# The up product of layer 0 at the front of the program, and a second early part of the output projection

## The chip, the cores and the metric

The kernel runs on one core of one Trainium2 chip. A core has TensorE (PE: matmuls, and PEld: the loads of their stationary operands), VectorE (DVE), ScalarE (ACT), GpSimd (POOL) and SyncE (SP, which here issues most DMAs); matmuls write to PSUM, everything else lives in SBUF. The metric is the device time of one execution in microseconds (us), as the median of several.

## The reference

One step of a two-layer encoder trunk over 1024 prompt tokens and 32 sample tokens, 1024 channels wide. Layer 0 is a Mamba-2 mixer (in projection, causal convolution, chunked scan in 8 groups, gate, group norm, output projection), layer 1 latent attention. Behind each mixer stands a term of per-layer embeddings p:

```
hn = rmsnorm(h, ln_w)                       # layer 0: the input x
proj = hn @ in_w                            # z, x/B/C, dt of the scan
y = ssd_scan(...) ; y = rmsnorm((y + D*xs) * silu(z))     # per group
h = h + y @ out_w
g = sigmoid(rmsnorm(h, norm_w) @ gate_w)
h = h + (p[i] @ up_w) * g
```

The product `p[0] @ up_w` ("the up product of layer 0") depends on inputs alone. Its result is first used when the gate of layer 0 is known.

## The kernel before

All tensors are held channel by token: 128 channels on the partitions, tokens along the free dimension. A product of two fp32 tensors is made of three matmuls: each operand is split into a high part h (rounded to the type fp32r, ScalarE or VectorE) and a low part l (the rest, VectorE or GpSimd), and `gemm` (L209) runs wh x ah, wh x al, wl x ah for every block of 128 channels. A weight block is loaded and split by `load_weight` (L192): a DMA into the tile `wraw`, `wh` by a cast (on ScalarE, or on VectorE where `eng_h` is given), `wl` by a subtraction on GpSimd. Each of these three tiles has two buffers in this stage.

**The order.** The program is written in Python in one order, but a planner at build time, with a model of the durations, orders the instructions of each engine by their readiness, an earlier line going first where two are ready; a tile whose buffers are all taken waits until one comes free. On the chip each engine then runs its own list in that fixed order and waits by semaphores.

**The scan stage** is `phase_ssd` (L263 to L580). At its front the input is normalized in three pieces of 384, 384 and 292 tokens (`TILES1`, index j). For each piece: four DMAs of the input into `xt` (L289), squares on ScalarE, VectorE and GpSimd, pairwise sums on VectorE (L303), four sums over the channels on TensorE (`psn`, L304), the inverse root on ScalarE (L182 and L183), then for each of eight channel blocks the product `hf` on VectorE (L311), its high part `hh` on ScalarE (L313) and its low part `hl` on GpSimd, or VectorE for two blocks of eight (L314). With j=0 also come the constants and the first two weights, `dtW` and `inW[0]` (L292), and some matmuls on constants (`busy`, L279) which only keep TensorE at work.

Then `raw_block` (L326) and `mblock` (L316) run the in projection: for each j one product of eight channel blocks for each weight, into one of three PSUM banks of the tag `mm`; ScalarE copies each out (L330). The first call takes `dtW` and `inW[0]` together (L350 and L351): "the first block". The dt chain on VectorE (L353 to L400) follows from it. After that 8 groups are scanned, with the in projections of the next group between them; `gate` (L417) forms y times silu(z) of a group, `finish` (L520) its norm: squares, sums, the root (L535) on ScalarE, the scaled y on VectorE (L538), and the store of y to DRAM (`y_d`, blocks 2g and 2g+1).

**The end of the stage** in the last group (L570 to L578): `up_product` (L229) is a generator. Its first step loads the two halves of `pT0` (128 x 1056 each) into `upr` and splits them into `upx` (tag `raw`, four of six buffers). Each further step takes one of 8 blocks of output channels: a weight (two loads of `upW0` serve four blocks each, nb=4), three pieces of 352 tokens with six matmuls each, a copy of each by ScalarE into `upe` (L252) and a store to `u_d` (L253). Its first step stands before the last gate and `finish`, the rest behind them (`run(up)`, L578).

**The output projection** is `phase_out` (L622), for two halves of 528 tokens. It loads the y of 16 channel blocks (`yraw`, L630) and splits them into `yhl`. `first` = 3 output columns are begun early, in the cuts that `early` gives: with `(8,)`, all three do blocks 0 to 8, then each of the 8 columns does what it still lacks. `part` (L643) loads the weights of a column in two halves, at block 0 and at block 8, and takes `[a - u : b - u]` of the half. Its PSUM tile `pso` spans two banks and has three buffers.

Of the kernel before, what the change touches and what calls it, by code (L numbers as in the profile page):

```python
# [10 lines left out]
F32 = mybir.dt.float32  # L11
F32R = mybir.dt.float32r
# [5 lines left out]
P = 128  # L18

T1 = 1060  # L20
RAWB = 6
# [3 lines left out]
T = 1056  # L25
# [166 lines left out]
def load_weight(c, src, nk, m, scale=None, eng_h=None, wp=None):  # L192
    nc = c.nc
    wp = wp or c.wp
    raw = wp.tile([P, nk, m], F32, tag="wraw", name="wraw")
    nc.sync.dma_start(raw, src)
    if scale is not None:
        nc.gpsimd.tensor_tensor(raw, raw, bc_last(scale, m), op=ALU.mult)
    wh = wp.tile([P, nk, m], F32R, tag="wh", name="wh", bufs=c.whb)
    wl = wp.tile([P, nk, m], F32R, tag="wl", name="wl", bufs=c.whb)  # L200
    if eng_h:
        eng_h.tensor_copy(wh, raw)
    else:
        nc.scalar.activation(wh, raw, AF.Copy)  # L204
    nc.gpsimd.tensor_tensor(wl, raw, wh.bitcast(F32), op=ALU.subtract)  # L205
    return wh, wl
# [19 lines left out]
    return c.pv[:rows, o + i : o + i + n]  # L226


def up_product(c, i, piece, raw, tiles, ps_tile, evac, nb=1):  # L229

    nc, I = c.nc, c.I
    o, n = piece
    acts = []
    for k in range(2):
        x = raw()[:, :n]
        nc.sync.dma_start(x, I[f"pT{i}"][:, k, o : o + n])
        h, l = tiles()[:, :n], tiles()[:, :n]
        split(c, h, l, x)
        acts.append((h, l))
    yield  # L240
    na = -(-n // 512)
    w_ = n // na
    for m in range(8):
        b = m % nb
        if b == 0:
            ws = load_weight(c, I[f"upW{i}"][m // 4][:, 2 * (m % 4) : 2 * (m % 4 + nb)], 2 * nb, P)
        w = [x[:, 2 * b : 2 * b + 2] for x in ws]
        u = evac()
        for a in range(na):
            ps = ps_tile()  # L250
            gemm(c, ps[:, :w_], w, acts, slice(w_ * a, w_ * a + w_))
            nc.scalar.activation(u[:, w_ * a : w_ * a + w_], ps[:, :w_], AF.Copy)  # L252
        c.store(c.u_d[i][m][:, o : o + n], u[:, :n])  # L253
        yield
# [8 lines left out]
def phase_ssd(c, ctx):  # L263
    nc, tc, I, O = c.nc, c.tc, c.I, c.O
# [12 lines left out]
    kp = es.enter_context(tc.tile_pool(name="keep", bufs=1))  # L277
    with tc.tile_pool(name="xin", bufs=2, side="right") as xp:
        def busy(x, k):  # L279

            ps = pc.tile([P, 512], F32, tag="trx", name="busy")
            for _ in range(k):
                nc.tensor.matmul(ps[:, : x.shape[-1]], c.ones, x, start=True, stop=True)

        busy(c.ones, 10)
        for j, (o, n) in enumerate(TILES1):
            xt = xp.tile([P, 8, n], F32, tag=f"xt{j}", name=f"xt{j}", bufs=1)
            for q in range(4):
                nc.sync.dma_start(xt[:, 2 * q : 2 * q + 2, :], I["xT"][:, 2 * q : 2 * q + 2, o : o + n])  # L289
            if j == 0:  # L290
                c.load_constants()
                early = [load_weight(c, I["dtW"], 8, 32, eng_h=nc.vector), load_weight(c, I["inW"][0], 8, P, eng_h=nc.vector)]  # L292
            ps = pc.tile([P, 512], F32, tag="st", name=f"psn{j}")
            for q in range(4):
                sq = [xp.tile([P, n], F32, tag="sq", name=f"sq{j}_{q}", bufs=6) for _ in range(2)]
                nc.scalar.activation(sq[0], xt[:, 2 * q], AF.Square)
                if j and q % 2:
                    nc.gpsimd.tensor_tensor(sq[1], xt[:, 2 * q + 1], xt[:, 2 * q + 1], op=ALU.mult)
                elif j == 0:
                    nc.vector.tensor_tensor(sq[1], xt[:, 2 * q + 1], xt[:, 2 * q + 1], op=ALU.mult)  # L300
                else:
                    nc.scalar.activation(sq[1], xt[:, 2 * q + 1], AF.Square)
                nc.vector.tensor_tensor(sq[0], sq[0], sq[1], op=ALU.add)  # L303
                nc.tensor.matmul(ps[:, :n], c.ones, sq[0], start=q == 0, stop=q == 3)  # L304
            r = xp.tile([P, n], F32, tag="r", name=f"r{j}")
            rsqrt(nc, c, r, ps[:, :n], 1.0 / 1024, c.eps)
            if j == 0:
                busy(r, 2)
            for k in range(8):
                hf = xp.tile([P, n], F32, tag="hf", name=f"hf{j}_{k}", bufs=3)  # L310
                nc.vector.scalar_tensor_tensor(hf, xt[:, k], pvc(c, "lnw0", k), r, op0=ALU.mult, op1=ALU.mult)  # L311
                hh, hl = hn[j][0][k], hn[j][1][k]
                nc.scalar.activation(hh, hf, AF.Copy)  # L313
                (nc.vector if k % 4 == 1 else nc.gpsimd).tensor_tensor(hl, hf, hh.bitcast(F32), op=ALU.subtract)  # L314

    def mblock(*blocks, ws=None):  # L316

# [237 lines left out]
    for g in range(G):  # L555
        scan_group(g, Ss[g])
        if g + 1 < G:
            bc_blocks(g + 1)
        if g:
            gate(g - 1, 0, Ss[g - 1])  # L560
            gate(g - 1, 1, Ss[g - 1])
        if g + 1 < G:
            x_block(g + 1, 0)
        else:
            gate(g, 0, Ss[g])
        if g:
            finish(g - 1, Ss[g - 1])
        if g + 1 < G:
            x_block(g + 1, 1)
        else:  # L570
            up = up_product(c, 0, (0, T), lambda: kp.tile([P, T1], F32, tag="cx", name="upr", bufs=6),
                            lambda: kp.tile([P, 3 + T1], F32R, tag="raw", name="upx", bufs=RAWB),
                            lambda: mm.tile([P, 512], F32, tag="mm", name="mm"),
                            lambda: kp.tile([P, T1], F32, tag="cx", name="upe", bufs=6), 4)
            next(up)
            gate(g, 1, Ss[g])
            finish(g, Ss[g])
    run(up)  # L578
    nc.sync.dma_start(O["conv_o"], conv_c.rearrange("p b s k -> p b (s k)"))
    es.close()  # L580

# [40 lines left out]
def phase_out(c, src_d, W, nkb, res, hpool, tmp, ypool, pool, first, early):  # L622

    nc = c.nc
    hs, rs = [], []
    for hf, (o, n) in enumerate(HB):
        acts = []
        for k in range(nkb):
            raw = pool.tile([P, 528], F32, tag="yraw", name="yraw", bufs=RAWY)
            nc.sync.dma_start(raw, src_d[k][:, o : o + n])  # L630
            yh, yl = (op_tile(ypool, (hf * nkb + k) % 16 < 8) for _ in range(2))
            split(c, yh, yl, raw)
            acts.append((yh, yl))
        row = []
        acc = tmp.tile([P, 528], F32, tag="acc", name="acc", bufs=2)

        group = range(0 if hf else first)
        cuts = [0, *early, nkb]
        pss = {m: mm2(c, "pso") for m in group}

        ws = {}

        def part(m, a, b):  # L643

            u = a // 8 * 8
            if a == u:
                ws[m] = load_weight(c, W[m][:, u : u + 8], 8, P)
            gemm2(c, pss[m], [x[:, a - u : b - u] for x in ws[m]], acts[a:b], first=a == 0, last=b == nkb)

        for a, b in zip(cuts[:-2], cuts[1:]):  # L650
            for m in group:
                part(m, a, b)
        for m in range(8):
            if m in group:
                part(m, *cuts[-2:])
            else:
                pss[m] = mm2(c, "pso")
                for u in range(0, nkb, 8):
                    part(m, u, u + 8)
            ps = pss[m]  # L660
            xr = pool.tile([P, 528], F32, tag="xres", name="xres", bufs=2)
            nc.sync.dma_start(xr, res[m][:, o : o + n])
            h = pool.tile([P, 528], F32, tag="hf", name="hf", bufs=2)
            nc.vector.tensor_tensor(pair(h), ps[:, :, :264], pair(xr), op=ALU.add)
            hh = hpool.tile([P, 528], F32R, tag="hH", name="hH", bufs=16)
            hl = hpool.tile([P, 528], F32R, tag="hL", name="hL", bufs=16)
            split(c, hh, hl, h)
            sumsq(c, tmp, h, acc, m == 0)
            row.append((hh, hl))
        hs.append(row)  # L670
        rs.append(lambda acc=acc: norm_r(c, tmp, acc, 1024, "r"))
    return hs, rs
# [451 lines left out]
def run(*gens):  # L1124
    for g in gens:
        for _ in g:
            pass
# [177 lines left out]
def build(tc, nc, I, O, dbg=None, ngroups=8, upto=9):  # L1305
# [4 lines left out]
    with ctx:  # L1310
# [61 lines left out]
        yp = ((ypa, 16), (ypb, 17))  # L1372
        tmp, tmp_es = pool("tmpA", "right")
        hp, hp_es = pool("hp")
        hs, rs = phase_out(c, c.y_d, I["outW"], 16, I["xres"], hp, tmp, yp, yt, 3, (8,))
        h1s = [[None] * 8 for _ in range(2)]
        accs = [None, None]

# [107 lines left out]
```

## Time and profile before

| | us |
|---|---|
| runs shown: median (lowest to highest) of 3 | 2014.39 (2013.51 to 2020.8) |
| the profiled execution | 2012.76 |
| its span, first to last instruction | 2011.0 |
| mean granted TensorE clock | 0.989 of full speed |

The profile is that of one execution; all durations below are from it. A group's row reads: line, engine, operation, output <- inputs, shapes, count | busy us, mean ns of one | idle time of the engine just before them, and what ended it. A row of the timeline reads: start, duration, engine, line, operation, tiles, count, and in brackets the engine's idle time before it with what ended it. Durations of matmuls are modelled and overlap, so TensorE's rate is read from the distance of their starts.

### The profile page before, as it was taken

To read this page: it belongs to the slowest core of one execution; us is meant where nothing else is said; L and a number is where in the kernel's file an instruction comes from. 1 tells how busy PE (TensorE), PEld (TensorE's weight loads), DVE (VectorE), ACT (ScalarE), POOL (GpSimd) and SP (SyncE) were. 2 spreads that over 40 slices of the span, in tenths; PEclk is the share of its full clock that TensorE was granted. 3 is DMA by queue.
4 is the path that set the end of the run, shared out by engine and by line. 5 is a ranking of instruction groups with operands and counts; after the bars stand their busy time and mean duration, and the time that the engine had idled before them with its cause. 6 is when DMAs were issued, how large, how long until landed. Compare 5 with 4: busy or idle time off the path is not lost. (4 is left out here: it accounts for less than half of the span.)

```text
span 2011.0 us, 32658 instructions
## 1 busy us (share of the span) xinstructions
PE 1932.2 (96%) x12871; PEld 1773.9 (88%) x12871; DVE 1282.6 (64%) x1601; ACT 1023.8 (51%) x1757; POOL 971.6 (48%) x813
## 2 busy tenths in 40 slices
PE   7989999999999999999998999999899999999999
PEld 5989899999999998999998999777777777779999
DVE  7898575858576675443267534274688787986544
ACT  4444444453545457334243432587687877754331
POOL 5433334344444444454678443122545453645772
PEclk8999999999999999999999999999999999999999
DMA  3143333334242446544333312533512221315432
GB/s 130 53 94 90 85 91 77 86 99 99 73 104 64 104 109 214 178 140 161 100 114 119 94 55 85 164 105 96 118 47 72 54 66 36 108 59 193 127 126 74
DMA packets 110730, 204.27 MB, mean 102 GB/s; under 512 B 18224, under 2 KB 60720, under 8 KB 110448
## 3 DMA queue, kind: packets, MB, share of 16 engines
q1 hardware_dynamic: 105472, 193.17, 32.5%
q0 software_dynamic: 2800, 6.91, 1.9%
q8 instruction: 101, 1.65, 0.3%
q10 hardware_dynamic: 2304, 2.10, 0.3%
q14 instruction: 53, 0.43, 0.1%
HBM read 156.81 MB, written 38.83 MB: 97 GB/s over the span
## 5 line engine op out<-in xcount | busy, mean ns | idle before, releaser
L205 POOL TENSOR_TENSOR wl<-wraw,wh 128x1024 fp32r<-128x1024 f32 (+2 forms) x185 | 374.1, 2024 | 413.7 <-ACT wh L204 371.5
L215 PE MATMUL mm<-hh,wh 128*128 128x384 f32 (+3 forms) x1176 | 386.0, 329 | 4.7 <-ACT raw L330 4.5
L215 PE MATMUL mm<-hl,wh 128*128 128x384 f32 (+3 forms) x1176 | 387.6, 330 | 0.0
L215 PE MATMUL mm<-hh,wl 128*128 128x384 f32 (+3 forms) x1176 | 385.4, 328 | 0.0
L204 ACT ACTIVATE wh<-wraw 128x1024 fp32r<-128x1024 f32 (+3 forms) x183 | 159.1, 869 | 280.8 <-PE pso L215 117.8
L215 PE MATMUL pso<-yhl,wh 128*128 128x264 f32 x1536 | 283.5, 285 | 5.6 <-ACT upe L252 2.9
L215 PEld LDWEIGHTS pso<-yhl,wh 128*128 128x128 f32 x1536 | 239.8, 189 | 7.0 <-DVE yhl L221 3.8
L215 PEld LDWEIGHTS mm<-hh,wh 128*128 128x128 f32 (+1 forms) x1176 | 220.3, 187 | 8.9 <-ACT raw L330 5.2
L215 PEld LDWEIGHTS mm<-hl,wh 128*128 128x128 f32 (+1 forms) x1176 | 220.8, 188 | 4.6 <-issue 2.4
L215 PEld LDWEIGHTS mm<-hh,wl 128*128 128x128 f32 (+1 forms) x1176 | 220.5, 187 | 4.2 <-issue 1.9
L215 PE MATMUL pso<-yhl,wl 128*128 128x264 f32 x768 | 219.3, 286 | 4.1 <-POOL wl L205 4.1
L413 DVE SCALAR_TENSOR_TENSOR cx<-raw,pv,cx 128x1060 f32<-128x1060 f32 x96 | 132.6, 1381 | 88.3 <-ACT cx L411 87.6
L215 PE MATMUL psi<-yhl,wh 128*128 128x264 f32 (+1 forms) x896 | 167.0, 287 | 3.9 <-ACT yhl L220 3.8
L215 PEld LDWEIGHTS pso<-yhl,wl 128*128 128x128 f32 x768 | 145.2, 189 | 4.7 <-POOL wl L205 4.7
L488 POOL TENSOR_TENSOR hm<-hT,cd_all 128x256 f32<-128x256 f32 x64 | 67.6, 1057 | 165.5 <-DVE hT L490 100.7
L215 PE MATMUL pg<-hH,wl 128*128 128x264 f32 x512 | 145.9, 285 | 0.7 <-POOL wl L205 0.7
L215 PE MATMUL pg<-hH,wh 128*128 128x264 f32 x512 | 145.9, 285 | 0.0
L215 PE MATMUL pg<-hL,wh 128*128 128x264 f32 x512 | 145.7, 285 | 0.0
L215 PEld LDWEIGHTS psi<-yhl,wh 128*128 128x128 f32 (+1 forms) x896 | 138.2, 185 | 5.6 <-ACT yhl L220 4.0
L1238 PE MATMUL st<-qk 128*128 128x512 f32 (+2 forms) x576 | 139.8, 358 | 0.9 <-ACT pf L1244 0.5
L215 PE MATMUL psi<-yhl,wl 128*128 128x264 f32 (+1 forms) x448 | 129.6, 289 | 1.1 <-POOL wl L205 1.1
L1259 POOL TENSOR_TENSOR pl<-pf,ph 128x512 fp32r<-128x512 f32 x64 | 81.3, 1271 | 102.1 <-DVE ph L1258 93.5
(517 smaller groups left out, 4579.0 us busy)
## 6 DMA issues: line engine op xcount, KB each, us to landing
wraw<-in_inW SPq DMA_DIRECT2D x48, 512.0 KB, 3.5
ex<-acs_d SPq DMA_DIRECT2D x32, 512.0 KB, 5.2
wraw<-in_outW SPq DMA_DIRECT2D x32, 512.0 KB, 3.6
yraw<-y_d SPq DMA_DIRECT2D x32, 264.0 KB, 4.6
u<-u_d SPq DMA_DIRECT2D x32, 264.0 KB, 2.8
eb<-ea_d SPq DMA_DIRECT2D x64, 128.0 KB, 4.0
y_d<-y SPq DMA_DIRECT2D x16, 512.0 KB, 2.9
wraw<-in_gateW SPq DMA_DIRECT2D x16, 512.0 KB, 3.6
```

The source lines that it names most:

```text
L204: nc.scalar.activation(wh, raw, AF.Copy)
L205: nc.gpsimd.tensor_tensor(wl, raw, wh.bitcast(F32), op=ALU.subtract)
L215: c.nc.tensor.matmul(ps, ww[:, k, :m], aa, start=first and k == 0 and i == 0, stop=last and k == n - 1 and i == 2)
L413: nc.vector.scalar_tensor_tensor(xh, raw[:, k : k + T1], pvc(c, "cw", 4 * b + k), xh, op0=ALU.mult, op1=ALU.add)
L488: nc.gpsimd.tensor_tensor(hm.rearrange("p (h q) -> p h q", q=64), hT.rearrange("p (h q) -> p h q", q=64), bc_last(cd_all[:, hs, ch], 64), ...
L1238: nc.tensor.matmul(ps[:, :n], a_[:, ks], b_[:, q], start=t == 0, stop=t == 2)
L1259: (nc.gpsimd if idx in L_POOL else nc.vector).tensor_tensor(pl[:, :n], pf[:, :n], ph[:, :n].bitcast(F32), op=ALU.subtract)
```

## The change

The first step of the up product (its loads and splits, and now also both loads of its weights, cast on VectorE) moves to the front, behind the constants and in the place of the loads of `dtW` and `inW[0]`. The rest of it is run behind the normalization, and only then are `dtW` and `inW[0]` loaded, now cast on ScalarE. The end of the stage no longer holds any of it. The output projection of layer 0 gets a second early cut: blocks 8 to 14 of its three first columns stand behind blocks 0 to 8, and blocks 14 and 15, the y of the last group, stand alone.

```diff
-def up_product(c, i, piece, raw, tiles, ps_tile, evac, nb=1):
+def up_product(c, i, piece, raw, tiles, ps_tile, evac, nb=1, weights=None):
...
-            ws = load_weight(c, I[f"upW{i}"][m // 4][:, 2 * (m % 4) : 2 * (m % 4 + nb)], 2 * nb, P)
+            ws = weights.pop(0) if weights else load_weight(c, I[f"upW{i}"][m // 4][:, 2 * (m % 4) : 2 * (m % 4 + nb)], 2 * nb, P)
...
             if j == 0:
                 c.load_constants()
-                early = [load_weight(c, I["dtW"], 8, 32, eng_h=nc.vector), load_weight(c, I["inW"][0], 8, P, eng_h=nc.vector)]
+                up = up_product(c, 0, (0, T), lambda: kp.tile([P, T1], F32, tag="cx", name="upr", bufs=6),
+                                lambda: kp.tile([P, 3 + T1], F32R, tag="raw", name="upx", bufs=RAWB),
+                                lambda: mm.tile([P, 512], F32, tag="mm", name="mm"),
+                                lambda: kp.tile([P, T1], F32, tag="cx", name="upe", bufs=6), 4,
+                                [load_weight(c, I["upW0"][i], 8, P, eng_h=nc.vector) for i in range(2)])
+                next(up)
...
                 (nc.vector if k % 4 == 1 else nc.gpsimd).tensor_tensor(hl, hf, hh.bitcast(F32), op=ALU.subtract)
+        run(up)
+        early = [load_weight(c, I["dtW"], 8, 32), load_weight(c, I["inW"][0], 8, P)]
...
         else:
-            up = up_product(c, 0, (0, T), lambda: kp.tile([P, T1], F32, tag="cx", name="upr", bufs=6),
-                            lambda: kp.tile([P, 3 + T1], F32R, tag="raw", name="upx", bufs=RAWB),
-                            lambda: mm.tile([P, 512], F32, tag="mm", name="mm"),
-                            lambda: kp.tile([P, T1], F32, tag="cx", name="upe", bufs=6), 4)
-            next(up)
             gate(g, 1, Ss[g])
             finish(g, Ss[g])
-    run(up)
...
-        hs, rs = phase_out(c, c.y_d, I["outW"], 16, I["xres"], hp, tmp, yp, yt, 3, (8,))
+        hs, rs = phase_out(c, c.y_d, I["outW"], 16, I["xres"], hp, tmp, yp, yt, 3, (8, 14))
```

## The prediction

> **What bounds the kernel now.** First the page: busy shares, then the 40 slices (50 us each).
>
> ```profile
> PE 1932.2 (96%) x12871; PEld 1773.9 (88%) x12871; DVE 1282.6 (64%) x1601; ACT 1023.8 (51%) x1757; POOL 971.6 (48%) x813
> PE   7989999999999999999998999999899999999999
> PEclk8999999999999999999999999999999999999999
> ```
>
> TensorE sets the time. It is below nine tenths in four slices only, and the first of them, 0 to 50 us, is the emptiest. The scan stage ends in the sixteenth and seventeenth, which show a 9 each. So a product that is only moved gains nothing by itself: the gain is the idle or slowly clocked TensorE time that it fills at its new place, less what opens at its old one. Next, both places in the view by stretches. Its columns: length, then busy time (and instructions) of PE, PEld, DVE, ACT, POOL, then granted clock, DMA share, GB/s.
>
> ```profile
> 10.00:15.00 5.00, 2.09 (x6) 0.89 (x6) 4.79 (x4) 3.00 (x7) 4.03 (x4) 1.00 1.07 369
> 15.00:20.00 5.00, 2.08 (x3) 0.93 (x4) 4.96 (x6) 2.83 (x7) 4.07 (x4) 0.54 0.93 342
> 20.00:25.00 5.00, 5.00 (x15) 3.48 (x15) 5.00 (x8) 2.17 (x5) 2.46 (x3) 0.50 0.00 0
> 66.00:76.00 10.00, 10.00 (x63) 10.00 (x62) 8.57 (x7) 2.72 (x4) 5.83 (x5) 1.00 0.12 39
> 775.00:815.00 40.00, 34.14 (x210) 32.93 (x211) 15.24 (x13) 32.94 (x57) 16.62 (x11) 0.96 0.84 304
> ```
>
> At the front VectorE is full while it normalizes the input; TensorE has little to do, and from 15 to 25 us runs at half clock. At the end ScalarE carries 32.94 us of 40, and TensorE is idle for 5.9. What TensorE waits for up to 150 us (total, times, longest), and the rows of the two longest waits and of the first block's end:
>
> ```profile
> PE psn L304 <- DVE sq L303: 5.4, 5, 3.4
> PE mm L215 <- ACT raw L330: 4.3, 1, 4.3
> 16.55 1.65 PE L304 MATMUL psn<-sq,ones 128*128 128x384 f32 x2 [3.35 <-DVE sq L303]
> 46.70 0.47 ACT L330 ACTIVATE raw<-mm 128x384 f32<-128x384 f32 x1
> 47.22 0.45 PE L215 MATMUL mm<-hh,wh 128*32 128x292 f32 x1 [4.26 <-ACT raw L330]
> 56.23 0.34 PE L215 MATMUL mm<-hh,wh 128*128 128x384 f32 x1
> ```
>
> The 4.26 us are a PSUM bank whose copy stood on ScalarE behind the last normalization copies. At 56.23 the first block (dt and inW[0]) is through, and TensorE is full behind it (the stretch 66 to 76). I call this moment X; what delays X delays the rest.
>
> **The change, part by part. The moved product.** It has 8 x 3 x 6 = 144 matmuls of 352 columns. Every third one, at its old place:
>
> ```profile
> 791.39 0.33 PE L215 MATMUL mm<-upx,wl 128*128 128x352 f32 x1
> 791.87 0.33 PE L215 MATMUL mm<-upx,wl 128*128 128x352 f32 x1
> 792.36 0.32 PE L215 MATMUL mm<-upx,wl 128*128 128x352 f32 x1
> L252 ACT ACTIVATE upe<-mm 128x352 f32<-128x352 f32 x22 | 9.6, 469 | 1.3 <-PE mm L215 1.3
> ```
>
> 0.485 us for three is 0.162 each, so 144 take 23.3 us. That is the credit at the end. Its 24 copies out of PSUM (0.469 each, 11.3 us of ScalarE) move too.
>
> **When it can start.** SyncE issues xt0, the constants, the two halves of upW0, then the two halves of pT0, then xt1 and xt2.
>
> ```profile
> xt<-in_xT SPq DMA_DIRECT2D x8, 384.0 KB, 5.4
> pv<-in_pv SPq DMA_DIRECT2D x1, 166.5 KB, 5.0
> cst<-in_cst SPq DMA_DIRECT2D x1, 128.0 KB, 4.9
> bd<-in_bd SPq DMA_DIRECT2D x1, 128.0 KB, 4.8
> wraw<-in_dtW SPq DMA_DIRECT2D x1, 128.0 KB, 4.6
> 10.21 0.69 DVE L202 CAST wh<-wraw 128x1024 fp32r<-128x1024 f32 x1 [1.01 <-DMA wraw<-in_inW]
> 763.62 1.07 ACT L220 ACTIVATE upx<-upr 128x1056 fp32r<-128x1056 f32 x1
> 768.36 1.73 DVE L221 TENSOR_TENSOR upx<-upr,upx 128x1056 fp32r<-128x1056 f32 x1
> 46.06 1.68 POOL L314 TENSOR_TENSOR hl<-hf,hh 128x292 fp32r<-128x292 f32 x2 [0.88 <-ACT hh L313]
> ```
>
> Before, xt0, constants, dtW (128 KB) and inW[0] (512 KB) make 2.6 MB, there at 10.2. After, xt0, constants, 1024 KB of upW0 and 1056 KB of pT0 (128 x 1056 x 4 B twice) make 4.1 MB; at the 369 GB/s of the stretch from 10 to 15 us the last lands near 14. Two splits (1.07 on ScalarE, up to 1.73 on VectorE) follow, the first half earlier: TensorE starts in earnest at about 15. xt1 and xt2 land 4 us later (1.5 MB more ahead of them); VectorE gets about 3.9 us more (two splits of 1.73; its two casts of 0.69 take the place of those of dtW and inW[0], the smaller of which took 0.4 less), GpSimd two subtractions of 2.4 (row below). So the last hl comes at about 52 instead of 47.7. That is hidden as long as TensorE needs it later, as the sum below gives (X less the 6.5 us of j=2); uncovered, these 4 us would be paid in full. The 8 stores of u_d (4.3 MB) stand on SyncE's queue ahead of later weight loads, whose slots aren't free yet anyway, and move while DMA is at 0.00 (20 to 25 us): nothing.
>
> **What TensorE must do before X.**
>
> ```profile
> 12.00:56.20 44.20, 30.13 (x144) 22.21 (x145) 0.81 0.18 64
> L304 PE MATMUL psn<-sq,ones 128*128 128x292 f32 x8 | 2.3, 408 | 0.0
> ```
>
> The first row is line 215 alone (PE, PEld, clock, DMA): the first block's 144 matmuls, 30.1 us at clock 0.81. At full clock 63 fit in 10 us (the stretch from 66), though a few records may be missing; I take 0.161, so 23.2 us. The norm sums of j=2 take 2.3 and of j=1, by columns (384/292), 3.0. With the up product: 23.3 + 23.2 + 5.3 = 51.8, so X is at least 15 + 51.8 = 66.8. To this I add stalls. Their nearest row is the 5.4 us for norm sums, for these remain in TensorE's order between the up matmuls, and VectorE, which feeds them, is now later. The lower end is 0; the upper is 5.4 + 4.3 = 9.7. Of the 5.4 the longest wait, 3.4, ended at about 16.5, when the up product has hardly begun; I count it at half and take 3.7. So X = 70.5, a cost of 70.5 - 56.2 = 14.3 (10.6 to 20.3). Gained: the slow clock goes, as TensorE is then dense from 15 on. A loss below nothing (X under 66.8) I exclude, since no listed work goes away. dtW and inW[0] now need wh/wl slots that the up weights hold (two slots): dtW's comes free halfway, inW[0]'s at the end. Casting (1.06) and subtracting (2.4, row below) hide behind the dt product of j=0 and 1 (48 x 0.161 = 7.7); uncovered they cost 3.5, inside the upper end. The dt chain on VectorE is next late: it starts when dt of j=2 is through, with inW[0] of j=2 (24 matmuls of 292 columns, some 3 us) still ahead of X both times, so it shifts by the same amount and I give it nothing.
>
> **The scan's end.**
>
> ```profile
> L221 DVE TENSOR_TENSOR yhl<-yraw,yhl 128x528 fp32r<-128x528 f32 x8 | 8.6, 1120 | 4.7 <-ACT yhl L220 4.7
> L220 ACT ACTIVATE yhl<-yraw 128x528 fp32r<-128x528 f32 x8 | 5.2, 650 | 0.2 <-DMA yraw<-y_d 0.2
> L205 POOL TENSOR_TENSOR wl<-wraw,wh 128x1024 fp32r<-128x1024 f32 x2 | 4.8, 2404 | 1.0 <-ACT wh L204 1.0
> L204 ACT ACTIVATE wh<-wraw 128x1024 fp32r<-128x1024 f32 x2 | 2.2, 1078 | 2.7 <-PE mm L215 2.7
> 775.71 0.40 ACT L330 ACTIVATE raw<-mm 128x292 f32<-128x292 f32 x1
> 806.07 0.51 PE L215 MATMUL pso<-yhl,wh 128*128 128x264 f32 x2 [2.93 <-ACT upe L252]
> 808.52 2.56 DVE L538 SCALAR_TENSOR_TENSOR y<-y,pv,yr 128x1060 f32<-128x1060 f32 x2 [11.56 <-ACT yr L183]
> 809.87 2.17 SPq L170 DMA_DIRECT2D y_d<-y  x4
> 830.00:900.00 70.00, 70.00 (x581) 70.00 (x580) 28.96 (x20) 24.60 (x34) 39.25 (x18) 1.00 0.41 130
> yraw<-y_d SPq DMA_DIRECT2D x32, 264.0 KB, 4.6
> y_d<-y SPq DMA_DIRECT2D x16, 512.0 KB, 2.9
> ```
>
> The last gate product ends at about 775.5 (its copy starts at 775.71) and output products begin at 806.07. So 806.1 - 775.5 - 23.3 = 7.3 us are lost, and 1.6 to the clock (0.96 over these 40 us): 9. After the change only output products stand there. One matmul is 70/581 = 0.12 us. Blocks 0 to 8 of three columns are 144 matmuls, 17.3; blocks 8 to 14 of two columns are 72, 8.7: 26.0 of cover. The third column's second weights find both slots taken until a first part (14, 16) has run. ScalarE decides when the last group's y exists. At present VectorE gets its root at 808.5; ScalarE loses 11.3 us of copies, but gets six more splits (6 x 0.65 = 3.9) and two more weight casts (2.2) ahead of that point: 803.3. The store leaves 1.35 later and lands in 2.9, the load takes 4.6, the split 1.8 (0.65 + 1.12): 814. The y loads share DMA with u_d no longer (0.84 of its time now), for which I take off 1: 813. So 813 - 775.5 - 26.0 = 11.5 is lost, and 2.1 more while the third column's weights are made (1.08 + 2.4 less one part (14, 16), 12 x 0.12): 13.6. Less the 9 of today, the end costs 4.6. The low end is 0 (no other engine in the way, y 4 to 5 us earlier), the high end 9 (y as late as now).
>
> **A rule against the change.** The wait of 4.26 us above shows a PSUM copy held up by copies that stood ahead of it. The Trainium skill ("TensorE: Matmul & The Clock Gate", section "Architectural detail: the array is 16× 32×32, not 1× 128×128") says that ScalarE and VectorE are strict FIFO queues; the row agrees. By this rule taken to its end the sum would be that of the third rival, +11.9; by the rows alone it is the one below.
>
> **Sum.** -23.3 + 14.3 + 4.6 = **-4.4**, with ends of -23.3 + 10.6 + 0 = -12.7 and -23.3 + 20.3 + 9 = +6. It is made against the profiled execution (2012.76, of which 2011.0 is the span): 2008.4. The median of the runs shown (2014.39) lies 1.6 above that execution, so as a median I state **2010**; the times below are on that footing.
>
> **The rivals.** (1) The front fills cleanly: no stalls and an end that costs 1: -23.3 + 10.6 + 1 = -11.7, about 2002.7. For it: the clock of 0.50 shows how empty the front is. Against: the 5.4. (2) The end opens again: with two weight slots and a late y the fill runs out; end 9 with the front as forecast: 0.0, about 2014.4; the change then only moves an idle time without shortening it. For it: ScalarE's 32.94 of 40. Against: it loses 11.3. (3) Slower: on ScalarE the up copies stand between normalization copies that wait for VectorE, so with three PSUM banks the up product lasts as long as the normalization. If it ends with it (52), X is 52 + 23.2 = 75.2, the total 19.0 + 4.6 - 23.3 = +0.3: from there on the change loses. With half of the up product still to do then (11.6) it is +11.9, about 2026. For it: the 4.26 us. Against: ScalarE is only half busy there (2.17 to 3.00 of 5).
>
> **How the numbers follow.** Forecast 0.50, (1) 0.25, (2) 0.14, (3) 0.11. Range 1999 to 2018: it takes in (1), (2) and the first half of (3). A measurement of this kernel tells about 0.5%, 10 us, from no change. Faster by more than that (under 2004.3): most of (1) and the quick edge of the forecast, 0.27. Slower by more: the far half of (3), 0.06. Between: 0.67.
>
> **What would show it.** Up matmuls from about 15 us at clock near 1; X near 70; PE waits at the front for norm sums or for copies of upe (few: rival 1; on copies over 8 us: rival 3). At the end TensorE idle for some 4 us behind the last gate product and a second gap ahead of the blocks 14 and 15 (over 8 us: rival 2). The forecast is wrong if the up product is put behind the first block after all, or if other parts of the program change their length by more than 3 us.

## The result and the profile after

The changed kernel takes 2037.49 us (median of 4, 2034.17 to 2039.17) against 2014.18 (median of 4) for the kernel before on the same chip. The ratio of the means is 1.0106, 95% interval 1.0082 to 1.0131: 21 us more, between 16.5 and 26.4 by the interval. The forecast was 2010, with a range of 1999 to 2018: it had the wrong sign, and about the length of the moved product (23.3 us) came on top instead of staying hidden. The page of the changed kernel, busy shares and two of the rows of 40 slices:

```profile
PE 1938.0 (95%) x12871; PEld 1776.8 (87%) x12871; DVE 1288.3 (63%) x1601; ACT 1023.0 (50%) x1757; POOL 969.8 (48%) x813
PE   7999999999999996999999999999899999999999
PEclk9999999999999998899999999999999999999999
```

TensorE does the same 12871 matmuls. The first slice, which the product was to fill, still shows a 7, and a 6 has opened in the sixteenth (763 to 814 us), where a 9 stood. Both places by stretches, columns as before:

```profile
10.00:15.00 5.00, 1.56 (x4) 0.68 (x4) 4.59 (x5) 2.42 (x5) 3.13 (x2) 1.00 1.03 397
15.00:20.00 5.00, 0.74 (x3) 0.46 (x3) 4.96 (x4) 1.20 (x3) 4.53 (x3) 0.79 1.07 366
20.00:25.00 5.00, 3.05 (x10) 2.60 (x10) 5.00 (x5) 4.48 (x9) 4.42 (x4) 0.53 0.48 161
...
800.00:805.00 5.00, 0.00 (x0) 0.00 (x0) 2.35 (x2) 4.97 (x7) 2.34 (x1) 0.50 0.95 339
805.00:810.00 5.00, 0.00 (x0) 0.00 (x0) 4.47 (x7) 1.26 (x3) 2.92 (x1) 0.50 0.93 332
810.00:815.00 5.00, 0.69 (x1) 0.29 (x1) 1.25 (x2) 2.65 (x5) 3.41 (x3) 0.50 0.49 157
815.00:820.00 5.00, 2.06 (x3) 0.86 (x3) 1.51 (x2) 2.99 (x6) 2.61 (x4) 0.50 0.55 162
```

At the front TensorE is no fuller than before from 10 to 25 us (before 2.09, 2.08 and 5.00 of 5; now 1.56, 0.74 and 3.05). At the end of the stage it stands empty for 10 us and nearly so for 10 more, at a granted clock of 0.50. The timeline of the changed kernel shows why it is empty at the front:

```profile
5.37 1.50 SPq L236 DMA_DIRECT2D upr<-in_pT  x2
...
13.62 1.58 ACT L318 ACTIVATE hh<-hf 128x384 fp32r<-128x384 f32 x3 [2.54 <-DVE hf L316]
...
15.10 1.07 ACT L220 ACTIVATE upx<-upr 128x1056 fp32r<-128x1056 f32 x1
...
16.23 0.74 PE L215 MATMUL mm<-upx,wh 128*128 128x352 f32 x3 [3.54 <-ACT upx L220]
...
19.98 0.52 ACT L318 ACTIVATE hh<-hf 128x384 fp32r<-128x384 f32 x1 [3.81 <-DVE hf L316]
20.39 1.25 DVE L221 TENSOR_TENSOR upx<-upr,upx 128x1056 fp32r<-128x1056 f32 x1
20.41 1.07 ACT L220 ACTIVATE upx<-upr 128x1056 fp32r<-128x1056 f32 x1
...
21.70 0.66 PE L215 MATMUL mm<-upx,wh 128*128 128x352 f32 x1 [4.72 <-DVE upx L221]
...
22.84 2.06 DVE L221 TENSOR_TENSOR upx<-upr,upx 128x1056 fp32r<-128x1056 f32 x1
```

Both halves of pT0 are issued by 6.9 and land a median of 7.3 us after their issue, so they are there at about 14, as forecast. But they are split by the engines that normalize the input. On ScalarE each split (L220) stands behind copies `hh` (L318) that had waited 2.54 and 3.81 us for VectorE's `hf`; on VectorE the two subtractions (L221) stand between normalization products. The last ends at 24.90. (This is the strict order of a queue which the Trainium skill states, "TensorE: Matmul & The Clock Gate", section "Architectural detail: the array is 16× 32×32, not 1× 128×128"; these rows agree with it.) The rows that end the front's steps, before and then after:

```profile
54.03 0.48 ACT L350 ACTIVATE xr<-mm,pv 32x292 f32<-32x292 f32 x1
```

```profile
52.47 1.71 POOL L319 TENSOR_TENSOR hl<-hf,hh 128x292 fp32r<-128x292 f32 x2 [0.88 <-ACT hh L318]
...
54.66 0.32 PE L215 MATMUL mm<-upx,wl 128*128 128x352 f32 x1
...
54.83 0.33 PE L215 MATMUL mm<-hh,wh 128*32 128x384 f32 x1
...
75.71 0.48 ACT L357 ACTIVATE xr<-mm,pv 32x292 f32<-32x292 f32 x1
...
77.91 0.34 PE L215 MATMUL mm<-hh,wh 128*128 128x384 f32 x1
```

The up product ends at 55, just behind the last `hl` (54.2), and the whole first block follows it: the last copy of the dt product (`xr`) comes at 75.71 instead of 54.03, **21.7 us later**; X is 77.9 instead of 56.2. The first dt matmul (54.83) follows the last up matmul at once, so the later weights cost nothing here, and from 55.0 to X lie 22.9 us, the first block's own work. At the end of the stage, waits of TensorE from 740 to 900 us (total, times, longest), then the timeline:

```profile
PE psy L259 <- ACT ysh L220: 20.9, 3, 17.6
```

```profile
799.83 0.39 ACT L337 ACTIVATE raw<-mm 128x292 f32<-128x292 f32 x1
...
807.08 4.67 POOL L430 TENSOR_TENSOR y<-y,raw 128x1060 f32<-128x1060 f32 x1 [4.74 <-DVE raw L189]
...
814.31 0.69 PE L259 MATMUL psy<-ysh,ones_r 128*128 128x384 f32 x1 [17.60 <-ACT ysh L220]
...
822.01 0.61 PE L260 MATMUL psy<-ysl,ones_r 128*128 128x292 f32 x1 [0.27 <-POOL ysl L221]
822.42 0.64 PE L215 MATMUL pso<-yhl,wh 128*128 128x264 f32 x2
...
828.06 2.56 DVE L545 SCALAR_TENSOR_TENSOR y<-y,pv,yr 128x1060 f32<-128x1060 f32 x2 [11.55 <-ACT yr L183]
...
829.42 2.12 SPq L170 DMA_DIRECT2D y_d<-y  x4
...
839.50 0.71 DVE L221 TENSOR_TENSOR yhl<-yraw,yhl 128x528 fp32r<-128x528 f32 x1 [0.80 <-ACT yhl L220]
```

From the copy of the last z block (799.83) run the gate, the squares, the norm sums (`psy`), the root, the scaled y, its store, its load and its split, which ends at 840.21 for the last of the 16 blocks: a tail of 40.4 us. In TensorE's order the output products (`pso`) stand behind the last of the norm sums. So they begin 22.6 us after that copy, and all of that stays empty but for six short sums. Before, the same two points were 775.71 and 806.07: 30.4 us, of which the up product filled 23.3.

### The profile page after: what moved, and what is told of

Same layout as the page of the kernel before. It is cut to its first block, busy times and chain, and to the rows that moved or that the text cites. A ratio compares the mean times of both kernels' runs of the same rounds, so it can differ in the third digit from the quotient of the medians.

```text
span 2035.7 us, 32655 instructions
## 1 busy us (share of the span) xinstructions
PE 1938.0 (95%) x12871; PEld 1776.8 (87%) x12871; DVE 1288.3 (63%) x1601; ACT 1023.0 (50%) x1757; POOL 969.8 (48%) x813
```

## The experiments

Two theories were tested. **A**, on the end: this tail needs TensorE work that neither depends on the last group nor stands behind its norm sums; the up product was that work and cost next to nothing there, so taking it away gains next to nothing. (The first expectations put A as a matter of the PSUM banks; this wider form is what the runs with new banks left of it.) **C**, on the front: the product is charged nearly in full, as its operands are split late and the first block, which used that time before, now runs behind it. D is the rival at the front, as each expectation words it.

**The second cut undone** (changed kernel):

```diff
-        hs, rs = phase_out(c, c.y_d, I["outW"], 16, I["xres"], hp, tmp, yp, yt, 3, (8, 14))
+        hs, rs = phase_out(c, c.y_d, I["outW"], 16, I["xres"], hp, tmp, yp, yt, 3, (8,))
```

> The changed kernel with the second early cut taken back (blocks 14 and 15 no longer apart). Theory A (PSUM banks: the planner can place no output product ahead of the last norm sum of the scan, because the output pool takes the banks of both scan pools): the cut has nothing to fill, so within 4 us of the changed kernel, 2033 to 2041. Theory B (the two more weight casts and six more splits of the second cut hold up ScalarE and with it the last y): 5 to 10 us faster than the changed kernel, 2027 to 2032.

2035.86 us, ratio to before 1.0107 (1.0092 to 1.0123), against 1.0106 with the cut. The second cut makes no difference that these runs can tell: the work that was to replace the up product has no part in the result.

**The up product left out** (kernel before, its term `u` replaced by a load of other data of the same shape):

```diff
-            up = up_product(c, 0, (0, T), lambda: kp.tile([P, T1], F32, tag="cx", name="upr", bufs=6),
...
-            next(up)
...
-    run(up)
...
-            nc.sync.dma_start(u, c.u_d[i][m][:, o : o + n])
+            nc.sync.dma_start(u, (c.u_d[i] if i else I["xres"])[m][:, o : o + n])
```

> The kernel before without the up product of layer 0 (left out; the gate of layer 0 is multiplied with the residual input instead of u). It prices the credit of 23.3 us. Theory A: most of the up product's time at its old place was cover that nothing else can give; output products begin 22 us behind the last gate product instead of 30, so the time falls by 6 to 10 only, to 2004 to 2008. The rival, the prediction's own: output products take its place, the time falls by about 19 (23.3 less 4.6), to 1995.

2014.35 us, ratio 0.9999 (0.9989 to 1.0009): 23.3 us of TensorE work less, and no time less; the gain stayed below even what A expected. Its timeline:

```profile
774.69 0.39 ACT L330 ACTIVATE raw<-mm 128x292 f32<-128x292 f32 x1
...
797.28 0.64 PE L215 MATMUL pso<-yhl,wh 128*128 128x264 f32 x2
...
814.00 2.48 DVE L221 TENSOR_TENSOR yhl<-yraw,yhl 128x528 fp32r<-128x528 f32 x1 [0.77 <-ACT yhl L220]
```

The same 22.6 us from the z copy to the first output product as in the changed kernel. Of the 23.3 us, 15.5 reopen here at once (22.6, less the 30.4 - 23.3 = 7.1 lost before). The other 7.8 are still ahead at the first output product (797.28 against 806.07, 1.0 of it from earlier) and are gone in the total; see the last two runs. Against the run with one cut, which differs by the product at the front and what goes with it (its loads and stores, the later casts of `dtW` and `inW[0]`), the **price of the front** is 2035.86 - 2014.35 = 21.5 us: 1.08% of 2014, plus or minus 0.18% with the two intervals added as squares.

**The norm of the last group left out as well** (no squares, norm sums, root or scaling for the last group; y is stored as the gate leaves it):

```diff
+        if g == G - 1:
+            for b in range(2):
+                c.store(c.y_d[2 * g + b][:, :1024], y[:, b, :1024])
+                c.store(c.y_d[2 * g + b][:, 1024:], y[:, b, SMP1:])
+            return
```

> The kernel before without the up product (as in e2_no_up) and without the norm of the last scan group, whose y is stored as the gate leaves it. Theory A, as the two runs with new banks leave it (the end is a chain of some 40 us from the last gate product through gate, norm, store, load and split, which needs that much other TensorE work beside it): output products start some 10 us behind the last gate product instead of 22.6 and find the last y in time, 12 to 18 us faster than without the up product alone, 1996 to 2002. The rival (loads and splits of the first y are what holds the output products): no more than 3 us faster, 2011 to 2015.

2001.47 us, ratio 0.9938 (0.9919 to 0.9958): 12.9 us under the run before, as A expected.

```profile
780.72 0.39 ACT L330 ACTIVATE raw<-mm 128x292 f32<-128x292 f32 x1
...
800.67 7.16 DVE L221 TENSOR_TENSOR yhl<-yraw,yhl 128x528 fp32r<-128x528 f32 x5 [0.79 <-ACT yhl L220]
```

From the z copy to the last split the tail lasts 27.1 us (780.72 to 807.83), against 41.8 in the run before (774.69 to 816.48). So the end of the stage is set by the tail: shortening it pays, emptying TensorE beside it does not. Without the norm the output products no longer stand behind its sums either; the next run shows that this alone gains nothing.

**Output products ahead of the norm sums** (changed kernel). `psy` of the last group and `pso` use the same PSUM banks, which is why they stand in that order. Here `psy` gets two banks of its own, the output projection six:

```diff
+    pc2 = es.enter_context(tc.tile_pool(name="ps_y", bufs=1, space=bass.MemoryType.PSUM))
+    pc = Pools(pc1, st=pc2, yf=pc2)
...
-        for (o, n), tag in zip(TILES1, ("st", "yd", "yf")):
+        for (o, n), tag in zip(TILES1, ("st", "yf", "st") if g == G - 1 else ("st", "yd", "yf")):
...
-        c.ps, ps_es = pool("psA", space=bass.MemoryType.PSUM)
+        psa, ps_es = pool("psA", space=bass.MemoryType.PSUM)
+        psn, psn_es = pool("psN", space=bass.MemoryType.PSUM)
+        c.ps = Pools(psa, n2=psn)
...
```

> The changed kernel with PSUM laid out otherwise: the norm sums of the last group use two banks that the output products do not, so the output pool waits for the other banks alone. Theory A: output products start behind the first y splits, about 9 us behind the last gate product instead of 22.6; then the last y is waited for some 5 us; 10 to 14 us faster than the changed kernel, 2023 to 2028. Theory B (y or the weights are what is late): no more than 3 us faster, 2034 to 2038.

2036.63 us, ratio 1.0110 (1.0093 to 1.0127). The expectation of A fell; that of B, that y is what is late, held. TensorE's timeline, and a stretch of this run:

```profile
804.52 0.81 PE L215 MATMUL pso<-yhl,wh 128*128 128x264 f32 x2 [6.49 <-ACT yhl L220]
...
829.11 0.30 PE L260 MATMUL psy<-ysl,ones_r 128*128 128x292 f32 x1
```

```profile
830.00:840.00 10.00, 2.71 (x20) 2.18 (x18) 5.15 (x3) 8.32 (x10) 2.62 (x1) 0.83 0.30 107
```

The output products do begin 18 us earlier. But now the norm sums stand between them, the last at 829.11 instead of 822.01, so the tail ends later: its last split is through at 849.32, 48.2 us behind its z copy (801.14) instead of 40.4. TensorE is empty for 7.3 of the 10 us from 830, and its waits from 740 to 900 us add up to 21.6 us, against 23.5 in the changed kernel. The 26.0 us of output work are shorter than the tail in either order. An order with each norm sum as soon as it is ready and output products only in the waits between them was not tried. The same layout of banks in the kernel before:

> The kernel before with the same layout of PSUM. Theory A: there the up product already covers all but 7 us of the same wait, so the layout gives 0 to 7 us: 2007 to 2014. Theory B: no change, 2012 to 2016.

2016.25 us, ratio 1.0000 (0.9990 to 1.0011): B's "no change"; the layout itself costs nothing.

**More cover beside the up product** (kernel before with the second cut alone):

> The kernel before with one line of the change alone: output blocks 8 to 14 of the three first columns stand behind blocks 0 to 8, the up product stays at the end of the stage. Theory A (the tail of the last group lasts about 41 us from its last gate product to its split y; up 23.3 and blocks 0 to 8 17.3 cover 40.6 of that already, so 8.7 more of cover have nearly nothing left to hide): 2011 to 2016, within 0.2% of the kernel before. Rival (the 5.9 us that TensorE still idles there are filled by the 8.7): 2006 to 2009.

2016.26 us, ratio 0.9998 (0.9985 to 1.0011): as A said; there was nothing left to fill.

**The operands of the up product first** (changed kernel; the loads of upW0 and pT0 ahead of those of the input and the constants):

```diff
-            xt = xp.tile([P, 8, n], F32, tag=f"xt{j}", name=f"xt{j}", bufs=1)
-            for q in range(4):
-                nc.sync.dma_start(xt[:, 2 * q : 2 * q + 2, :], I["xT"][:, 2 * q : 2 * q + 2, o : o + n])
             if j == 0:
-                c.load_constants()
                 up = up_product(...)
                 next(up)
+            xt = xp.tile([P, 8, n], F32, tag=f"xt{j}", name=f"xt{j}", bufs=1)
+            for q in range(4):
+                nc.sync.dma_start(xt[:, 2 * q : 2 * q + 2, :], I["xT"][:, 2 * q : 2 * q + 2, o : o + n])
+            if j == 0:
+                c.load_constants()
```

> The changed kernel with the loads and splits of the up product ahead of the loads of x, so that its operands are split before the normalization fills VectorE and ScalarE. Theory C (the front costs 21.7 us because the up product's operands, landed at 13.9, are split only at 15 to 25 behind normalization work): up matmuls from about 9.5, first block done at 68 instead of 77.9, 8 to 11 us faster than the changed kernel, 2026 to 2030. Theory D (the third rival: the up product ends when the normalization ends, whenever it starts): the normalization ends 6 us later, the first block at 83, 4 to 6 us slower, 2041 to 2044.

2030.57 us, ratio 1.0083 (1.0068 to 1.0098).

```profile
48.26 0.32 PE L215 MATMUL mm<-upx,wl 128*128 128x352 f32 x1
...
70.04 0.48 ACT L358 ACTIVATE xr<-mm,pv 32x292 f32<-32x292 f32 x1
```

The product begins at 8 us and ends 6.4 earlier, and the last `xr` comes 5.7 earlier: late operands are a part of the price, but 16.0 of the 21.7 stay. C had expected 8 to 11 us; 5 (by the ratios) to 7 (by the medians) came. D's loss did not come: the last `hl` is at 54.9, against 54.2 in the changed kernel.

**Six PSUM banks for the up product** (changed kernel):

```diff
+                banks = itertools.cycle(("mm", "mm", "mm", "yd", "yf", "trb"))
...
-                                lambda: mm.tile([P, 512], F32, tag="mm", name="mm"),
+                                lambda: (lambda t: (mm if t == "mm" else pc).tile([P, 512], F32, tag=t, name="mm"))(next(banks)),
```

> The changed kernel with six PSUM banks in turn for the up product instead of three, so that TensorE can run three pieces further ahead of ScalarE's copies. Theory C: only the waits for copies of upe (2.5 us at the front) can go, 0 to 2.5 us faster, 2034 to 2038. Theory D (the copies tie the up product to the normalization): the up product ends at about 48 instead of 54.7, 5 to 7 us faster, 2030 to 2033.

2033.16 us, ratio 1.0095 (1.0078 to 1.0112); the product ends at 51.3 instead of 55.0 and the last `xr` is at 72.78, 2.9 earlier. No wait for copies of `upe` is left, where the changed kernel has 2.5 us. That lies between what C and D expected: banks are a term, but a small one.

**Half of the product at the front, half at the old place** (changed kernel; pT0 is loaded and split twice):

```diff
-    for m in range(8):
+    for m in ms:
...
-                                [load_weight(c, I["upW0"][i], 8, P, eng_h=nc.vector) for i in range(2)])
+                                [load_weight(c, I["upW0"][i], 8, P, eng_h=nc.vector) for i in range(1)], range(4))
...
+            up = up_product(c, 0, (0, T), ..., 4, None, range(4, 8))
+            next(up)
...
+    run(up)
```

> The changed kernel with the product split in two: output channels 0 to 3 (72 matmuls, one half of upW0) at the front, channels 4 to 7 at the old place, for which both halves of pT0 are loaded and split a second time; both early cuts kept. Theory A+C (the front charges nearly what it is given, 21.5 x 1/2 = about 11, and the end, with 11.7 of up and 26.0 of output blocks, covers 37.7 of some 41 us, so it charges 0 to 4): 2023 to 2029. Rival H (the idle 12 us of TensorE in the first 25 us take the first half free and only the second half was charged): 2012 to 2016.

2020.08 us, ratio 1.0019 (1.0005 to 1.0034): between the two expectations. Its timeline at the front:

```profile
38.94 0.32 PE L215 MATMUL mm<-upx,wl 128*128 128x352 f32 x1
...
52.08 1.68 POOL L319 TENSOR_TENSOR hl<-hf,hh 128x292 fp32r<-128x292 f32 x2 [0.88 <-ACT hh L318]
...
61.76 0.48 ACT L357 ACTIVATE xr<-mm,pv 32x292 f32<-32x292 f32 x1
```

11.7 us of product delay the last `xr` by 7.7. But the up product is through at 39, long before; was TensorE still what held the first block? The last `hl` is at 53.8, 6 us later than before. Hence one more run.

**The same half, with its operands first:**

> The kernel of the run before (output channels 0 to 3 at the front, 4 to 7 at the old place) with the loads and splits of pT0 and of the one upW0 half ahead of the input's loads instead of behind them. In the run before, the first half delayed the last copy of the dt product by 7.7 us (54.0 to 61.8) for 11.7 us of product, so 4 us of the front's idle time were used. Theory C (the front's idle TensorE time lies before 25 us and only operands split early reach it): the product runs from 8 us, the last copy of dt comes at 55 to 58, and the time is 2012 to 2016, equal to before or up to 3 us under it. Theory D (the input, landing later, delays the normalization as much as the product gains): last copy of dt at 60 to 63, time 2018 to 2022 as in the run before.

2019.84 us, ratio 1.0034 (1.0022 to 1.0046).

```profile
27.93 0.32 PE L215 MATMUL mm<-upx,wl 128*128 128x352 f32 x1
...
52.27 1.67 POOL L320 TENSOR_TENSOR hl<-hf,hh 128x292 fp32r<-128x292 f32 x2 [0.88 <-ACT hh L319]
...
54.60 0.45 PE L215 MATMUL mm<-hh,wh 128*32 128x292 f32 x1 [3.88 <-ACT xr L358]
...
60.06 0.48 ACT L358 ACTIVATE xr<-mm,pv 32x292 f32<-32x292 f32 x1
```

C fell here, D held. The product ends 11 us earlier than in the run before, at 28, in time that TensorE had free, and still the last `xr` is 6.0 us later than in the kernel before. So is the last `hl`: 53.94 against 47.74. Only behind it come the copies for which TensorE waits 3.88 us at 54.60, as it waited 4.26 at 47.22 in the kernel before. The front has **two limits**. With the whole product TensorE's own work comes last. With half of it, early, the normalization does, which the product's loads (1.5 MB more ahead of the input's) and splits delay by 6.2 us. With the loads behind the first piece of the input instead, in the run before, the last `hl` was as late (53.8). How the 6.2 divide between DMA and the engines was not tried.

**Where the 7.8 us go.** In the first trace of before, the program from the first matmul of layer 0's gate (`g`, behind the output projection) to the end lasts 1009.3 us; without the up product 1014.5. Both were run once more.

> The kernel before, once more, for a second trace. In its first trace the program from the first gate product to the end lasted 1009.3 us (2011.0 less 1001.7), in the one without the up product 1014.5, in the one with two cuts alone 1014.7. If this length is a matter of the execution: anything from 1008 to 1016 here. If the kernel before is really 5 us shorter there than a kernel without the up product: 1008 to 1010.

> The kernel without the up product, once more, for a second trace of the same length: anything from 1008 to 1016 if it is a matter of the execution, 1013 to 1016 if it belongs to the kernel.

1010.1 and 1013.5 (2009.5 less 999.4, 2012.7 less 999.2): each near its first trace, so 3 to 5 us of the 7.8 go behind that point. Against a property of the kernel speaks the run with the second cut alone: its instructions there stand in the order of before, and its trace has 1014.7. And in this second pair the lead is already gone at that first matmul (0.1 us, 7.6 in the first pair), where the two traces without the up product lie 5 us apart (994.1 and 999.2). Over all 14 traces that last part takes 1008.0 to 1010.1 in four (both of before and the two with new banks) and 1012.7 to 1016.0 in the other ten; no cause was found. Where the 7.8 go **stays open**. The medians say only that nothing of them is left.

## Why the prediction was wrong, step by step

- **What bounds the kernel**: right. TensorE sets the time, and a moved product is worth only the idle time that it fills at its new place less what opens at its old one.
- **The credit at the end** (-23.3) and **the end's cost** (+4.6, ends 0 and 9): this failed, and with it the sign. The length of the tail was nearly right: 37.5 us worked out (775.5 to 813), 40.4 measured. Wrong was the step "After the change only output products stand there ... 26.0 of cover", which counts that cover from 775.5 on. The products stand behind the last norm sum in TensorE's order, so the first 22.6 us have no cover at all; what opens is 15.5 at that place, and with what is lost later, of which 7.8 are not placed, the whole 23.3 (left out: ratio 0.9999). Order is not all of it: put ahead of the sums, the same products delayed the tail and gained nothing (1.0110). The second gap, ahead of blocks 14 and 15, never came: the cover left over at 822.42 (26.0) is longer than what the tail still lacks (17.8).
- **The front's cost** (+14.3, ends 10.6 and 20.3): measured 21.5 by the times and 21.7 by `xr`, above the upper end. Right were the mechanism (TensorE's work up to X) and, nearly, the work itself (51.8): 25 + 51.8 is 76.8, against X = 77.9. (Some 13 up matmuls, 2.1 us, ran before 25, and 2.5 us of waits for copies came behind it; the two nearly cancel.) Mis-sized was the start, "TensorE starts in earnest at about 15". The data landed as worked out (near 14); their splits were priced at their own duration, 1.07 and 1.73, and not at their place in two queues with other work ahead of them. They were through at 24.9, and from 15 to 25 the clock was again 0.79 and 0.53, where the sum had it gone.
- **The later `hl`**: 52 forecast, 54.2 measured; hidden, as said, as long as TensorE is later. The half product with its operands first shows its price when uncovered: 6.0, where 4 was written.
- **The third rival** had the right place, and its 19.0 for the front is near 21.7. That the up product ends (55) with the last `hl` is chance, though: with its operands first it ends at 48.6, and the last `hl` comes at 54.9. And what it blamed first, copies of `upe`, is 2.5 us of waits; the splits of `upx` are 8.5 (two rows, 5.0 and 3.5):

```profile
PE mm L215 <- DVE upx L221: 5.0, 2, 4.7
PE mm L215 <- ACT upx L220: 3.5, 1, 3.5
PE mm L215 <- ACT upe L252: 2.5, 3, 1.1
```

- **The second rival** named what happened at the end, but held it to 9, "y as late as now", for it counted idle time only up to y and not what stands in front of the fill. Either one alone gives about 0 in the working (0.0 and +0.3, or +11.9 with half of the product still to do); that both could come together, and that the end could cost all of the credit, had no place in it, so slower by 10 us got 0.06.
- **The range**: its top, 2018, lay below the sum's own upper end (2014.4 + 6 = 2020.4). The result lies above both.
- **The sign of being wrong** that the prediction named last did come: from the first matmul of layer 0's gate to the end the changed kernel takes 1013.8 us (2035.7 less 1021.9) against 1009.3, 4.5 longer. That part was not touched by the change, and the difference is the one left open above.

## What to carry to other kernels

Before work is moved out of a stretch, ask what the stretch lasts without it: where a chain of other engines' work lasts as long, the work is nearly free there, and a kernel that simply leaves it out shows this at once. Work that is to fill a gap must stand ahead of the gap's wait in the engine's own order, without holding up the chain itself, and its operands must be made by engines whose queues aren't full just then; count the place in the queue, not the duration. At the start of this program, the idle TensorE time beside a full VectorE was the normalization's latency: what was put there delayed the normalization by its loads and splits.

## What was not expected of the hardware

One operation of VectorE took 0.55 or 1.36 us at one shape, in the normalization of the changed kernel. VectorE, then GpSimd in the same stretch:

```profile
15.97 1.36 DVE L319 TENSOR_TENSOR hl<-hf,hh 128x384 fp32r<-128x384 f32 x1
...
25.92 0.55 DVE L319 TENSOR_TENSOR hl<-hf,hh 128x384 fp32r<-128x384 f32 x1
```

```profile
14.21 2.70 POOL L319 TENSOR_TENSOR hl<-hf,hh 128x384 fp32r<-128x384 f32 x2 [1.05 <-ACT hh L318]
16.88 2.65 POOL L205 TENSOR_TENSOR wl<-wraw,wh 128x1024 fp32r<-128x1024 f32 x1
...
27.63 1.71 POOL L319 TENSOR_TENSOR hl<-hf,hh 128x384 fp32r<-128x384 f32 x1 [2.04 <-ACT hh L318]
```

The long one lies beside GpSimd's two-operand operations, the short one in the 2.04 us in which GpSimd waits. The Trainium skill ("SBUF — State Buffer", section "SBUF: two separate sides") says that the two engines share a pair of ports which one instruction holds alone; the rows agree, though no run here takes GpSimd away. It bears on the front: VectorE's splits of `upx`, priced at up to 1.73, took 1.25 and 2.06 in this stretch.
